# Three prices of the planner's TensorE clock in a two-layer hybrid decoder kernel

## Chip, core and metric

The kernel runs on one core of a Trainium2 chip. The metric is the time of one execution on the device, in microseconds (us); the median of three runs before the change is 1532.54 us.

## What is computed

Two layers over a sequence of 2048 positions and 1024 channels in float32, each of the form x + RMSNorm(mixer(RMSNorm(x))):

```
layer 0:  q,k,v,ga,u,gb = split(h @ w_in)
          ya = sliding_window_attention(q,k,v,sinks) * silu(ga)     # window 128, 8 query heads on 2 kv heads
          yb = multiscale_pool(u) * silu(gb)                        # trailing windows 2, 4, 8, 16
          y  = concat(ya, yb) @ w_out
layer 1:  a,b,gate = split(h @ w_in)                                # 3 x 1024 columns
          glu  = a * sigmoid(b)
          conv = causal_depthwise_conv(glu, 31 taps per channel) + bias
          y    = (silu(layer_norm(conv)) * silu(gate)) @ w_out
```

## The kernel before

**Tiling.** Activations lie with channels on the 128 partitions and positions along the free axis. The sequence is worked in two halves of 1024 positions, a half in two blocks of 512. A weight tile holds 128 output channels against all 1024 input channels (8 tiles of 128 rows). To keep float32's precision with the faster float32r matmuls, weights and activations are split into a high and a low part; a projection of one weight tile on one block (`project`, line 378) is 8 x 3 = 24 matmuls of 512 columns: high times high, high times low, low times high. They sum in one of four "mm" banks of PSUM.

**Stages.** Layer 0, half 0: key, value, query and gate projections with attention beside them, pooling projections, then the output projection (`inproj0`, line 833; `outproj`, 942). The same for half 1. Then layer 1 for either half (`inproj1`, 1173): eight channel tiles with two weights each (the sigmoid's and its partner's), eight gate weights, the output projection. Loads run through SyncE's queue; ScalarE (ACT) makes the high part of a weight and VectorE (DVE) the low part (`w_split`, 348; tiles `wh`, `wl`). There are three buffers for raw weights and two for split ones. Large working tiles come from 37 slots of one tag, `s4`.

**The depthwise convolution.** Of the eight channel tiles, four (0, 1, 3, 5) are convolved on DVE (`conv_dve`, 1021): 31 taps, each one instruction over 1024 positions that multiplies by the channel's tap and adds to an accumulator; in the rows these are `s<-s,packed,s` with 128x1024 elements. The other four (2, 4, 6, 7) are convolved on TensorE (`conv_pe`, 1050): DVE builds a small banded weight tile of 640 elements (`s<-packed,ab`), and five plain float32 matmuls of 128 columns use it (`a<-s,s`, two records each in the trace); there are eight such groups per channel tile. Before that, DVE multiplies the two projections into the convolution's input (`glu`, 1102, `s<-t,mm`). When all eight are done, their sum is made on GpSimd, and a matmul with a tile of ones takes the mean over channels (`norm_block`, 1124, `a<-s,ones`); the layer norm, gate and split follow, and the output projection reads the result.

**What sets the order of the work.** Every engine works through its own queue in the order in which the program issues. This order is found while the program is built, by the class `Flow`. The main stream issues the projections. All else is background work, written as generators that run between the matmuls: `project` calls `flow.pump()` after every three matmuls. `Flow` keeps an estimated clock for each engine (P for TensorE, V for DVE, A for ACT, G, S); `Engine.cost` (lines 153 to 181) gives each instruction a price in us, and `note` advances the clock of its engine by that price, from the time at which its inputs are estimated to be there. `once` lets a background task make its next step under two conditions: the time that the task named as its earliest must lie 0.2 us (`MARGIN`) behind the TensorE clock, and, for a task of any priority but 0, neither the DVE nor the ACT clock may be over 1 us (`LAG`) ahead of the TensorE clock:

```
ready = task[3]
if ready is not None and ready + MARGIN > self.t["P"]:
    continue
if task[0] > 0 and max(self.t["V"], self.t["A"]) > self.t["P"] + LAG:
    continue
```

The DVE convolution is such a background task (priority 4) that offers one tap at a time:

```
for k in range(2, CK):
    yield flow.t["P"]
    r = acc[k % 2]
    V.scalar_tensor_tensor(r, gl[:, k:k + TH], dwn[:, slot, k:k + 1], r, op0=ALU.mult, op1=ALU.add)
```

Weight splits and gate products have priority 0; the convolution matmuls (priority 2) are issued once the TensorE clock has passed the estimated end of the tile that they read. Where the main stream needs something that is not there on the estimate, `wait` advances the TensorE clock. The estimate decides only the order; semaphores hold every real dependency. DVE's prices are 0.063 us + 0.067 us for a per-partition scalar + 1.04 ns per element (half that for plain copies and scalar operations from SBUF).

All instructions are issued through one helper, so that every row of the trace shows its line, L187; rows are told apart by tile names.

Of the kernel before, what the change touches and what calls it, by code (L numbers as in the profile page):

```python
# [49 lines left out]


class Flow:
    """Issues the program in an order that an estimate of each engine's clock suggests.

    Background work is written as generators ("tasks"). A task yields the estimated time at which
    its next step can start, or None when it waits for a buffer or for other tasks. The main stream
    feeds the tensor engine and lets tasks run between its matmuls. Tile draws every dependency;
    the estimate only decides the order of issue.
    """

    def __init__(self):
        self.t = {"P": 0.0, "V": 0.0, "A": 0.0, "G": 0.0, "S": 0.0}
# [7 lines left out]
    def keys(ap):  # L70
# [3 lines left out]
        return [(ap.name, c) for c in range(lo // 256, hi // 256 + 1)]  # L74

    def note(self, e, cost, ins, outs):
        s = self.t[e]
        for x in ins:
# [71 lines left out]
class Engine:  # L150
# [3 lines left out]
    def cost(self, op, out, ins, kw):  # L154
        n = 1
        for d in out.shape[1:]:
            n *= d
        psum = any(x.space == PSUM for x in ins + [out])
        ptr = 0.067 * sum(1 for x in ins if n > 1 and x.shape[-1] == 1)
        if self.key == "P":  # L160
            if op == "transpose":
                return 0.109
            f = ins[0].dtype
            if f == F32R:
                return max(0.107, 0.2148 * n / 512)
            if n * out.shape[0] < 256:
                return 0.108
            part = 0.56 if out.shape[0] == 64 else 1.0
            return part * n * 1.67e-3
        if self.key == "V":  # L170
            if op == "reciprocal":
                return 0.06 + n * 6.25e-3
            fast = op in ("tensor_copy", "tensor_scalar") and not psum
            return 0.063 + ptr + n * (0.52e-3 if fast else 1.04e-3)
        if self.key == "A":
            return (0.052 if psum else 0.093) + 1.4 * ptr + n * 0.833e-3 + (0.09 if kw.get("accum_out") is not None else 0.0)
        if kw.get("op") == ALU.pow:
            return 1.0
        if op == "tensor_tensor":
            return 0.1 + n * 2.2e-3  # L180
        return 0.1 + n * 3.4e-3
# [1122 lines left out]
```

## Time and profile before

| | |
|---|---|
| median of the runs | 1532.54 us (1532.35 to 1534.52) |
| span of the profiled execution | 1531.2 us |
| TensorE matmul, weight load | 1503.7 us, 1227.4 us busy |
| VectorE | 1232.9 us busy |
| ScalarE, GpSimd | 570.3 us, 97.7 us busy |
| instructions | 20024 |

The time of an execution is that of its span and what lies around it; the profiled execution's span is the only part that the profile shows. Busy time is the time in which an engine executes something; matmuls are pipelined, so that a mean of 395 ns for one does not say how often one starts. The granted clock is the share of TensorE's full speed (2.4 GHz) that the chip allowed. In a row of a group, the first number after the bar is busy time, the next the mean of one in ns, and after the second bar stands the engine's idle time just before instructions of that group, with what ended it.

### The profile page before, as it was taken

The numbers are of one execution on the slowest core, as the hardware profiler recorded it, in microseconds if no ns is written. First come the engines' busy times: TensorE is split into PE (matmuls) and PEld (weight loads), VectorE is DVE, ScalarE is ACT, GpSimd is POOL, SyncE is SP. The second block draws the span as 40 slices with busy tenths as digits, with TensorE's granted clock in tenths as the row PEclk, the third lists the DMA queues.
The fourth block names the chain that finished last, engine by engine and source line by source line (L and its number), as shares of the span: only waits on it lengthen the run. The fifth ranks groups of instructions, "written<-read, shape, count | busy, mean of one in ns | idle before, by whom it ended". The sixth has DMA issues, their size and how long they took to land.

```text
span 1531.2 us, 20024 instructions
## 1 busy us (share of the span) xinstructions
PE 1503.7 (98%) x7578; PEld 1227.4 (80%) x7578; DVE 1232.9 (81%) x1913; ACT 570.3 (37%) x1085; POOL 97.7 (6%) x83
## 2 busy tenths in 40 slices
PE   8999999999999999999999999999999999999997
PEld 6877788788877788788888888788888888778897
DVE  7888775787887664686999999887679999998555
ACT  6454432554434432553211121665421111136541
POOL 0000000000000000000202122100000101110000
PEclk9999999999999999999999999999999999999999
DMA  6122211463410011465222122125642122211254
GB/s 221 43 71 84 78 59 55 151 194 124 157 32 32 28 52 45 151 198 175 95 67 66 56 60 74 42 83 166 212 159 66 49 71 63 69 46 42 83 171 145
DMA packets 75695, 146.89 MB, mean 96 GB/s; under 512 B 8144, under 2 KB 31312, under 8 KB 75600
## 3 DMA queue, kind: packets, MB, share of 16 engines
q1 hardware_dynamic: 75600, 145.63, 30.3%
q8 instruction: 59, 0.97, 0.3%
q14 instruction: 36, 0.29, 0.1%
HBM read 118.33 MB, written 18.87 MB: 90 GB/s over the span
## 4 chain that ended last, share of the span: by engine, by line
PE 79%; DVE 16%; issue 3%; DMA 1%; ACT 1%; SPq 0%; POOL 0%; DVEq 0%; POOLq 0%; ACTq 0%
PE mm L187 67%; DVE s L187 14%; PE a L187 6%; PE pv L187 3%; PE pt L187 2%; DVE wl L187 2%; DMA wr<-in_wc 0%; ACT s L187 0%; SPq L187 0%; DMA s<-s 0%; POOL s L187 0%; DMA wr<-in_wa 0%; DVE t L187 0%; ACT wh L187 0%; DVE a L187 0%
## 5 line engine op out<-in xcount | busy, mean ns | idle before, releaser
L187 PE MATMUL mm<-s,wh 128*128 128x512 f32 (+1 forms) x3616 | 1134.3, 395 | 7.3 <-ACT s L187 6.4
L187 PEld LDWEIGHTS mm<-s,wh 128*128 128x128 f32 x3616 | 667.6, 189 | 155.6 <-ACT s L187 8.3
L187 PE MATMUL mm<-s,wl 128*128 128x512 f32 (+1 forms) x1808 | 709.3, 392 | 0.0
L187 PEld LDWEIGHTS mm<-s,wl 128*128 128x128 f32 x1808 | 340.2, 188 | 76.4
L187 DVE SCALAR_TENSOR_TENSOR s<-s,packed,s 128x1024 f32<-128x1024 f32 x232 | 300.9, 1356 | 0.0
L187 ACT ACTIVATE wh<-wr 128x1024 fp32r<-128x1024 f32 (+1 forms) x138 | 145.5, 1054 | 366.3 <-PE mm L187 343.2
L187 DVE TENSOR_TENSOR wl<-wr,wh 128x1024 fp32r<-128x1024 f32 (+1 forms) x138 | 168.0, 1217 | 106.6 <-ACT wh L187 105.3
L187 PE MATMUL a<-s,s 128*128 128x128 f32 (+2 forms) x944 | 131.5, 286 | 6.2 <-DVE s L187 6.1
L187 PEld LDWEIGHTS a<-s,s 128*128 128x128 f32 x944 | 119.9, 191 | 18.0 <-DVE s L187 10.5
L187 ACT ACTIVATE t<-mm 128x512 f32<-128x512 f32 (+1 forms) x122 | 68.7, 563 | 100.2 <-PE mm L187 100.2
L187 DVE TENSOR_TENSOR t<-t,t 128x512 f32<-128x512 f32 (+1 forms) x131 | 86.5, 665 | 18.5 <-ACT t L187 16.7
L187 ACT ACTIVATE s<-mm 128x512 f32<-128x512 f32 (+1 forms) x116 | 68.0, 586 | 57.9 <-PE mm L187 46.1
L187 ACT ACTIVATE s<-t 128x512 fp32r<-128x512 f32 (+1 forms) x52 | 48.9, 939 | 69.0 <-DVE t L187 68.6
L187 POOL TENSOR_TENSOR rs<-ms,mhalf 128x4 f32<-128x4 f32 (+1 forms) x21 | 23.7, 1127 | 731.5 <-DVE ms L187 731.5
L187 DVE TENSOR_TENSOR s<-t,s 128x512 fp32r<-128x512 f32 (+1 forms) x56 | 51.5, 919 | 21.3 <-ACT s L187 19.9
L187 ACT ACTIVATE t<-s 128x512 f32<-128x512 f32 x80 | 48.5, 629 | 52.5 <-DVE s L187 47.1
L187 DVE TENSOR_TENSOR s<-s,s 128x512 f32<-128x512 f32 (+3 forms) x84 | 64.2, 792 | 3.7 <-ACT s L187 2.8
L187 DVE TENSOR_TENSOR t<-pt,packed 128x512 f32<-128x512 f32 x64 | 44.1, 689 | 24.1 <-PE pt L187 23.8
L187 ACT ACTIVATE s<-s,st 128x128 f32<-128x128 f32 x128 | 49.8, 391 | 29.8 <-DVE st L187 29.7
L187 POOL TENSOR_TENSOR s<-s,s 128x1024 f32<-128x1024 f32 x14 | 42.3, 3019 | 285.3 <-DMA s<-t 191.9
L187 ACT ACTIVATE t<-a,packed 128x128 f32<-128x128 f32 x64 | 18.4, 371 | 108.2 <-PE a L187 97.7
L187 DVE TENSOR_TENSOR s<-packed,ab 128x640 f32<-128x640 f32 x64 | 51.6, 851 | 0.0
(104 smaller groups left out, 1018.6 us busy)
## 6 DMA issues: line engine op xcount, KB each, us to landing
wr<-in_wo SPq DMA_DIRECT2D x64, 512.0 KB, 3.5
wr<-in_wc SPq DMA_DIRECT2D x48, 512.0 KB, 3.5
wr<-in_wa SPq DMA_DIRECT2D x27, 512.0 KB, 3.6
xr<-in_xp SPq DMA_DIRECT2D x32, 256.0 KB, 4.0
x<-s SPq DMA_DIRECT2D x32, 256.0 KB, 3.1
xh<-x SPq DMA_DIRECT2D x32, 256.0 KB, 3.0
out_y<-s SPq DMA_DIRECT2D x32, 256.0 KB, 2.4
xr<-x SPq DMA_DIRECT2D x24, 256.0 KB, 3.9
```

The lines of the kernel that those rows point to most:

```text
L187: fn(*args, **kw)
```

## The change

Three prices of TensorE in `Engine.cost` change: a float32r matmul of n columns from 0.2148 x n/512 us (at least 0.107) to 0.007 + 0.224 x n/512 (at least 0.111), and a plain float32 matmul from 1.67 to 1.74 ns per column. The docstring of `Flow` becomes blank lines, so that line numbers stay. The instructions themselves, their sizes and their buffers are untouched.

```diff
--- before.py
+++ after.py
@@ -50,13 +50,13 @@
 
 
 class Flow:
-    """Issues the program in an order that an estimate of each engine's clock suggests.
-
-    Background work is written as generators ("tasks"). A task yields the estimated time at which
-    its next step can start, or None when it waits for a buffer or for other tasks. The main stream
-    feeds the tensor engine and lets tasks run between its matmuls. Tile draws every dependency;
-    the estimate only decides the order of issue.
-    """
+
+
+
+
+
+
+
 
     def __init__(self):
         self.t = {"P": 0.0, "V": 0.0, "A": 0.0, "G": 0.0, "S": 0.0}
@@ -162,11 +162,11 @@
                 return 0.109
             f = ins[0].dtype
             if f == F32R:
-                return max(0.107, 0.2148 * n / 512)
+                return max(0.111, 0.007 + 0.224 * n / 512)
             if n * out.shape[0] < 256:
                 return 0.108
             part = 0.56 if out.shape[0] == 64 else 1.0
-            return part * n * 1.67e-3
+            return part * n * 1.74e-3
         if self.key == "V":
             if op == "reciprocal":
                 return 0.06 + n * 6.25e-3
```

## Rows read from the trace of the kernel before

**Rows 1.** The page, busy us (share of the span) and instructions by engine.
```profile
PE 1503.7 (98%) x7578; PEld 1227.4 (80%) x7578; DVE 1232.9 (81%) x1913; ACT 570.3 (37%) x1085; POOL 97.7 (6%) x83
```

**Rows 2.** The page, chain that ended last, shares of the span by engine.
```profile
PE 79%; DVE 16%; issue 3%; DMA 1%; ACT 1%; SPq 0%; POOL 0%; DVEq 0%; POOLq 0%; ACTq 0%
```

**Rows 3.** Busy by stretch: span, PE, PEld, DVE, ACT, POOL, clock, DMA share, GB/s.
```profile
50.00:200.00 150.00, 149.95 (x903) 116.46 (x902) 128.79 (x379) 74.58 (x222) 2.58 (x5) 1.00 0.21 68
400.00:550.00 150.00, 149.38 (x900) 115.09 (x899) 117.37 (x345) 61.60 (x182) 2.15 (x4) 1.00 0.12 39
736.30:955.60 219.30, 216.56 (x1103) 181.79 (x1102) 217.20 (x195) 38.50 (x69) 37.10 (x20) 1.00 0.24 65
...
1140.80:1360.20 219.40, 215.99 (x1091) 180.24 (x1090) 214.57 (x188) 36.32 (x67) 21.43 (x10) 1.00 0.23 64
```

**Rows 4.** PE's waits, whole run: us in total, times, longest us.
```profile
PE mm L187 <- ACT s L187: 6.4, 3, 5.6
PE a L187 <- DVE s L187: 6.3, 12, 1.3
PE a L187 <- POOL s L187: 2.3, 2, 1.2
```

**Rows 5.** PE's timeline, projections only, 24 matmuls from first to last: start, us.
```profile
599.81 0.39 PE L187 MATMUL mm<-s,wl 128*128 128x512 f32 x1
...
605.36 0.40 PE L187 MATMUL mm<-s,wl 128*128 128x512 f32 x1
```

**Rows 6.** The chain in order of time: start, us, one convolution run of 40 records.
```profile
791.71 4.46 PE a L187 x40
```

**Rows 7.** DVE groups by form, 736.3 to 955.6 us.
```profile
L187 DVE SCALAR_TENSOR_TENSOR s<-s,packed,s 128x1024 f32<-128x1024 f32 x116 | 150.6, 1354 | 0.0
L187 DVE TENSOR_TENSOR s<-packed,ab 128x640 f32<-128x640 f32 x32 | 26.9, 885 | 0.0
L187 DVE TENSOR_TENSOR wl<-wr,wh 128x1024 fp32r<-128x1024 f32 x16 | 19.5, 1222 | 0.6 <-ACT wh L187 0.5
L187 DVE SCALAR_TENSOR_TENSOR s<-t,mm 128x512 f32<-128x512 f32 x14 | 12.3, 880 | 1.3 <-PE mm L187 1.2
L187 DVE TENSOR_SCALAR s<-s,packed 128x1024 f32<-128x1024 f32 x7 | 7.3, 1073 | 0.0
L187 DVE TENSOR_TENSOR s<-s,s 128x1024 f32<-128x1024 f32 x3 | 6.1, 2027 | 0.1
L187 DVE TENSOR_TENSOR t<-t,t 128x512 f32<-128x512 f32 x2 | 1.4, 702 | 0.1
L187 DVE TENSOR_TENSOR s<-s,xr 128x512 f32<-128x512 f32 x2 | 1.3, 710 | 0.0
```

**Rows 8.** PE groups by form, 736.3 to 955.6 us.
```profile
L187 PE MATMUL mm<-s,wh 128*128 128x512 f32 x517 | 161.8, 394 | 0.0
L187 PE MATMUL mm<-s,wl 128*128 128x512 f32 x258 | 101.5, 394 | 0.0
L187 PE MATMUL a<-s,s 128*128 128x128 f32 x320 | 38.3, 277 | 2.7 <-DVE s L187 2.7
```

**Rows 9.** PE groups by form, 1140.8 to 1360.2 us.
```profile
L187 PE MATMUL mm<-s,wh 128*128 128x512 f32 x514 | 161.5, 395 | 0.0
L187 PE MATMUL mm<-s,wl 128*128 128x512 f32 x257 | 101.4, 394 | 0.0
L187 PE MATMUL a<-s,s 128*128 128x128 f32 x320 | 38.2, 277 | 3.4 <-DVE s L187 3.4
```

**Rows 10.** DVE groups by form, 1140.8 to 1360.2 us, taps and gate products.
```profile
L187 DVE SCALAR_TENSOR_TENSOR s<-s,packed,s 128x1024 f32<-128x1024 f32 x116 | 150.3, 1359 | 0.0
...
L187 DVE SCALAR_TENSOR_TENSOR s<-t,mm 128x512 f32<-128x512 f32 x14 | 12.6, 903 | 4.6 <-PE mm L187 4.6
```

**Rows 11.** PE's timeline after the start: start, us; the first 17 matmuls end here.
```profile
13.14 1.05 PE L187 MATMUL mm<-s,wh 128*128 128x512 f32 x2
...
14.42 1.02 PE L187 MATMUL mm<-s,wh 128*128 128x512 f32 x2
```

## The prediction

> **What bounds the kernel now.** First the shares by engine: TensorE (PE) is busy 1503.7 of 1531.2 us, VectorE (DVE) 1232.9 [rows 1]. The chain of waits then runs through PE for 79% of the span and through DVE for 16% [rows 2], so DVE sets the pace somewhere. The busy times by stretch say where: from 736.3 to 955.6 us DVE is busy 217.20 of 219.3 us, from 1140.8 to 1360.2 us 214.57 of 219.4; in the two attention stretches it has 128.79 and 117.37 of 150 [rows 3]. These two stretches, the depthwise convolution of each half, are where both engines are full, cut from its first tap on DVE to the last sum. The waits of PE, last, are small over the whole run: 6.4 us for ACT (5.6 of it in one wait, the start's) and 6.3 us for DVE tiles [rows 4]. A better order could win back little; a worse one can lose much.
>
> The profiled execution's span is 1531.2 us against a median of 1532.54: 1.3 us lie outside the span or between executions, and I add them at the end.
>
> **The change part by part.** No instruction is added, removed or reshaped: the docstring goes, and three prices of the planner rise. What can change is where the background work (DVE, ACT, DMA and their matmuls) stands among the main stream's matmuls.
>
> *The prices against the trace.* In a stretch of nothing but 512-column projections, 24 matmuls take 605.36 - 599.81 = 5.55 us, 0.231 us each [rows 5]. The old price is 0.2148, the new one 0.007 + 0.224 = 0.231: from 7% too low to right. A 128-column float32 matmul stands in the trace as two records; 40 records last 4.46 us, so 0.223 us for one [rows 6]; its price goes from 0.2138 to 0.2227, again right. So the change does what it says for PE.
>
> *The Trainium skill on this.* "TensorE: Matmul & The Clock Gate" (section "Wait — 56ns, not 53.3ns?") gives 215.7 ns from start to start for 512 columns, at the full clock; by it the old price would be the right one. This trace shows 0.231 us [rows 5], and a granted clock of 1.00 in every stretch of [rows 3], so the measurement decides; by the page's pace the term worked out below would be 60 x 0.2157 = 12.9 us where the trace gives 13.9.
>
> *The prices of DVE stay as they are, and they are too low.* A tap of the convolution (1024 elements, one per-partition scalar) is priced 0.063 + 0.067 + 1.065 = 1.195 us; 116 of them keep DVE busy 150.6 us, 1.298 each [rows 7]. The whole first convolution stretch at the planner's prices: 116 x 1.195 = 138.6; 32 weight builds of 640 elements x 0.729 = 23.3; 16 splits x 1.128 = 18.0; 14 gate products x 0.595 = 8.3; 7 first taps at about 0.70 = 4.9; 3 sums x 1.128 = 3.4; 4 of 512 elements x 0.595 = 2.4; together 198.9 us, for 217.2 us of real DVE time [rows 3, 7]. DVE is thus priced 8% too low.
>
> *Both clocks in that stretch.* PE has 517 + 258 = 775 projections and 160 convolution matmuls there [rows 8]: at the old prices 775 x 0.2148 + 160 x 0.2138 = 200.7 us. That is DVE's 198.9 within 1%. The second stretch: 514 + 257 = 771 projections, 160 others [rows 9], 199.8 us on PE's clock; DVE's counts there are those of the first but for one first tap and three short operations fewer [rows 10], where two of them stand, about 196.5 us. This equality is what the rule in `once` enforces: no background step is issued while DVE's clock is over 1 us ahead of PE's. There the throttle binds, and the planner hands out DVE work in exact proportion to its PE clock. Both clocks being 7 to 8% slow, their ratio was nearly right.
>
> *What the new price does there.* The same DVE work, 200.7 us of it with the idle on its clock, is now spread over 200.7 us of PE time at right prices: N x 0.231 + 160 x 0.2227 = 200.7, N = 715 in place of 775. In the order of issue 60 projections move from beside the convolution to behind it, 60 x 0.231 = 13.9 us of PE work; in the second half likewise 13.8. DVE still needs its 217 us. PE can't run ahead: convolution matmuls, and at the end the mean's matmul, are in its one queue at the place where the planner thinks that DVE is done, and each waits for a DVE tile; everything behind it waits too. So PE idles 14 us more per half. Its later work (gate projections, output projection) is as long as before plus the 60 projections, at full pace: nothing after the stretch gives the 14 us back, since PE is 98 to 100% busy there and the waits there are the mean's (2.3 us over both halves, for GpSimd's sum), which depend on DVE's end and not on the order.
>
> What can come off: DVE itself idles 2.1 us in the first stretch and 4.8 in the second [rows 3], mostly for PE's projections before a gate product (1.2 and 4.6) [rows 7, 10]. With DVE always the later one these waits can go, and the stage gets as much shorter. Bounds: 11.8 to 13.9 us for the first half, 9.0 to 13.8 for the second. I take the middle, 12.9 + 11.4 = 24.3 us.
>
> *The attention stretches* (50 to 200 and 400 to 550 us). The same background work now stands beside 7% fewer matmuls: some 140 us of PE in place of 150, in which DVE needs 128.8 and 117.4 us [rows 3]. On average it fits, so the lower bound is nothing. If DVE paced all 300 us, it would be 7% of them, 20 us. PE is busy 149.95 and 149.38 of 150 us there [rows 3], so it waits for nearly nothing now; the nearer end is the low one. I take 3 us for bursts in which the softmax steps run late.
>
> *Loads and the other stretches.* A planned DMA latency is worth 7% fewer matmuls now; the cover is the weight buffers (three raw, two split), and each weight is used for 24 or 48 matmuls, 5.5 or 11 us. Cost nothing; if a load came late the price would be 1 to 2 us once or twice. Below nothing: the start waits are for the first tile and lie ahead of any choice of order, so 1 to 2 us at most can be won outside the convolution. Both ends, -2 to +3, go into the range.
>
> Sum: 24.3 + 3 = 27.3; 1531.2 + 27.3 + 1.3 = 1559.8, rounded to 1560 us.
>
> **Rivals.** (a) *No change.* Buffers, not the throttle, hold the taps back (37 large slots), or the equality of the clocks is chance; then the order hardly moves: 1530 to 1535 us. For it: the code has such waits. Against: two stretches in which the clocks agree within 1 and 2%, while DVE has no idle to show for a missing buffer.
>
> (b) *Faster.* Right prices place the convolution matmuls so that PE meets finished tiles: the waits of PE for DVE in the stretches (2.7 and 3.4 us) [rows 8, 9] and the mean's 2.3 go, 8 us: 1524 us. It decides if DVE's true pace, and not its price, governed how far its work ran ahead of PE. Against it: PE waits for DVE already with the clocks in balance, and the change slows only PE's clock.
>
> (c) *Slower still, by attention*: DVE paces these stretches too, 20 us in place of 3: 1577 us. Its operations on 128 elements cost far more than their price; but PE shows almost no wait there now.
>
> (d) *Slower still, by the clock.* The 14 us per half come in lumps, since between the matmuls of one convolution channel on PE and the next lie up to four weights of 48 projections, 44 us: 8% of that is 3.5 us of idle. After the idle start the first 17 matmuls ran at the 1.2 GHz level, at (14.42 - 13.14) / 3 = 0.427 us [rows 11], 0.196 us over the full pace, 3.3 us in all. If every lump brought that back, a slow PE would only wait less at the next group, as DVE sets the pace; what stays is the last lump of each half: 7 us, 1567. The Trainium skill ("TensorE: Matmul & The Clock Gate", section "Why this matters for your kernels") has idle gaps between bursts bring the half clock back; the granted clock is 1.00 in all stretches of [rows 3], and PE's longest wait for DVE is 1.3 us [rows 4], so this trace shows neither such a gap nor its price.
>
> **How the numbers follow.** Forecast 0.72, (a) 0.09, (b) 0.07, (c) 0.06, (d) 0.06. A change under 0.2% (3 us) can't be told from none. Faster is (b), 0.07; same is (a), 0.09; the rest is slower, 0.84. The forecast's own range is 1551 to 1571: 20.8 us for both stretches with nothing from attention and 2 us won, up to 27.7 with 8 from attention and 3 from loads. To leave out no more than 2 in 10 I reach down to 1541, for a throttle that binds for part of the stretch only, and up to 1577 for (c) and (d).
>
> **What would show it.** Right: the convolution stretches keep DVE's busy time (about 217 and 215 us) and hold some 60 projections fewer each; PE's waits for DVE and its idle time there grow from 3 to about 14 us, ahead of convolution matmuls; the stages behind them grow in matmuls, not in waits. Wrong: counts of projections beside the taps as before (then (a)); longer waits between 50 and 200 us (then (c)); a granted clock under 1.00 between the convolution groups (then (d)); a shorter stretch with the same 116 taps would overthrow the working altogether.

## The result and the profile after

The changed kernel takes 1574.14 us (median; 1573.01 to 1575.61) beside 1532.66 for the kernel before in the same measurement: 2.7% slower, ratio 1.0269 with the interval [1.0254, 1.0283]. Forecast were 1560 us and a loss of 27; the loss is 41.5. Span of the profiled execution: 1573.8 us.

Busy times by engine and the chain's shares by engine, from the page of the changed kernel:
```profile
PE 1521.0 (97%) x7578; PEld 1236.8 (79%) x7578; DVE 1229.2 (78%) x1913; ACT 569.6 (36%) x1085; POOL 104.0 (7%) x83
...
PE 67%; DVE 24%; issue 4%; DMA 3%; ACT 2%; SPq 0%; POOL 0%; DVEq 0%; POOLq 0%; ACTq 0%
```
The instructions are the same in number [rows 1]; the chain runs through DVE for 24% of the span where it was 16% [rows 2].

Where the time went can be read from the main stream, whose order is fixed: the start of its nth projection matmul (counted from 0) in either trace (us, worked out from the start times):
```
projection   stands at                      before    after    late
 672         half 0's attention done          234.4    239.8     5.4
1824         half 1's attention done          558.3    569.0    10.7
2592         first taps of convolution 1      740.8    753.1    12.3
3552         behind convolution 1            1009.0   1037.2    28.1
4320         before convolution 2            1190.4   1218.7    28.3
5184         behind convolution 2            1437.4   1479.7    42.3
5711         the last                        1518.4   1560.8    42.4
```
So 10.7 us are lost with the two attention stretches, 1.6 more on the way to the first convolution, 15.8 and 14.0 in the convolutions, and nothing in between. Such differences hold to about 1 us: the start alone, up to the 48th projection, put two kernels whose layer 0 was left as before 0.9 us ahead in their traces.

The stretches of [rows 3] in the changed kernel (the convolutions from the first tap to the start of the last DVE sum, as there):
```profile
50.00:200.00 150.00, 147.27 (x880) 112.97 (x879) 122.40 (x366) 70.37 (x216) 2.54 (x5) 1.00 0.21 67
400.00:550.00 150.00, 147.58 (x887) 112.70 (x887) 113.62 (x349) 60.65 (x181) 1.41 (x3) 1.00 0.14 43
749.10:966.80 217.70, 207.19 (x1018) 173.93 (x1017) 212.33 (x194) 34.44 (x61) 41.18 (x19) 0.96 0.22 62
1168.80:1380.80 212.00, 200.70 (x989) 167.90 (x988) 207.98 (x184) 31.45 (x55) 18.55 (x9) 0.98 0.22 61
```
In the convolutions PE is now idle for 10.5 and 11.3 us, where it was 2.7 and 3.4, and its granted clock is under 1.00 for the first time. PE's longest waits over the run, answering [rows 4]:
```profile
PE a L187 <- DVE s L187: 25.1, 16, 4.6
PE mm L187 <- ACT s L187: 7.0, 3, 5.9
PE pt L187 <- DVE t L187: 2.4, 3, 1.5
PE a L187 <- POOL s L187: 2.2, 2, 1.1
...
PE pv L187 <- DVE t L187: 1.9, 5, 0.5
```
The first row is the change: convolution matmuls (`a`) waited 6.3 us for DVE's tiles and now wait 25.1, up to 4.6 at once. PE's groups in the first convolution, then in the second, to be held against [rows 8, 9]:
```profile
L187 PE MATMUL mm<-s,wh 128*128 128x512 f32 x474 | 149.9, 397 | 0.0
L187 PE MATMUL mm<-s,wl 128*128 128x512 f32 x238 | 94.4, 396 | 0.0
L187 PE MATMUL a<-s,s 128*128 128x128 f32 x298 | 41.0, 303 | 9.0 <-DVE s L187 9.0
```
```profile
L187 PE MATMUL mm<-s,wh 128*128 128x512 f32 x474 | 148.2, 394 | 0.0
L187 PE MATMUL mm<-s,wl 128*128 128x512 f32 x238 | 93.7, 394 | 0.0
L187 PE MATMUL a<-s,s 128*128 128x128 f32 x277 | 36.9, 297 | 11.3 <-DVE s L187 11.2
```
712 projections stand beside either convolution, where 775 and 771 stood; the forecast had 715 for the first. One of the waits, in PE's timeline (start, duration), and then the stretches of the wait and behind it (the granted clock is the third number from the end):
```profile
917.25 0.62 PE L187 MATMUL mm<-s,wh 128*128 128x512 f32 x2
917.71 0.40 PE L187 MATMUL mm<-s,wl 128*128 128x512 f32 x1
922.55 7.51 PE L187 MATMUL a<-s,s 128*128 128x128 f32 x40 [4.44 <-DVE s L187]
929.81 0.71 PE L187 MATMUL mm<-s,wh 128*128 128x512 f32 x2
```
```profile
917.70:922.40 4.70, 0.41 (x2) 0.00 (x0) 4.70 (x5) 0.00 (x0) 0.96 (x1) 0.91 0.41 70
922.40:928.40 6.00, 5.85 (x27) 5.85 (x28) 6.00 (x8) 0.00 (x0) 3.51 (x1) 0.50 0.24 87
```
PE has nothing to do for 4.4 us, the granted clock falls to 0.50, the 1.2 GHz level, and the 40 records behind the wait take 7.3 us instead of 4.46 [rows 6]. DVE is busy throughout.

The convolution does not end with the last DVE sum. Up to the mean's matmul, the two stages of the kernel before and then of the changed one:
```profile
736.37:960.21 223.84, 220.02 (x1117) 184.30 (x1115) 219.15 (x196) 39.72 (x71) 39.48 (x21) 1.00 0.23 64
1140.83:1364.86 224.03, 219.40 (x1105) 182.67 (x1103) 216.61 (x189) 36.29 (x67) 23.78 (x11) 1.00 0.23 63
```
```profile
749.15:976.86 227.71, 216.07 (x1067) 181.28 (x1065) 214.24 (x195) 36.07 (x66) 45.93 (x21) 0.96 0.22 60
1168.81:1397.35 228.54, 213.91 (x1066) 178.77 (x1064) 214.94 (x188) 34.23 (x64) 23.62 (x11) 0.98 0.22 59
```
The stages are 3.9 and 4.5 us longer, though they hold 50 and 40 projections fewer.

### The profile page after: what moved, and what is told of

It is laid out like the page before. It is cut to its first block, busy times and chain, and to the rows that moved or that the text cites. A ratio compares the mean times of both kernels' runs of the same rounds, so it can differ in the third digit from the quotient of the medians.

```text
span 1573.8 us, 20021 instructions
## 1 busy us (share of the span) xinstructions
PE 1521.0 (97%) x7578; PEld 1236.8 (79%) x7578; DVE 1229.2 (78%) x1913; ACT 569.6 (36%) x1085; POOL 104.0 (7%) x83
## 4 chain that ended last, share of the span: by engine, by line
PE 67%; DVE 24%; issue 4%; DMA 3%; ACT 2%; SPq 0%; POOL 0%; DVEq 0%; POOLq 0%; ACTq 0%
PE mm L187 55%; DVE s L187 20%; PE a L187 7%; PE pv L187 3%; PE pt L187 2%; DVE wl L187 2%; DVE t L187 2%; ACT s L187 1%; ACT t L187 1%; DMA xr<-in_xp 1%; DMA xh<-in_xn 0%; DMA xr<-x 0%; DMA s<-in_xn 0%; SPq L187 0%; DMA wr<-in_wc 0%
## 5 line engine op out<-in xcount | busy, mean ns | idle before, releaser
L187 DVE SCALAR_TENSOR_TENSOR s<-s,packed,s 128x1024 f32<-128x1024 f32 x232 | 293.3, 1328 | 0.0
L187 PE MATMUL a<-s,s 128*128 128x128 f32 (+2 forms) x944 | 142.6, 301 | 25.1 <-DVE s L187 24.3
L187 PEld LDWEIGHTS a<-s,s 128*128 128x128 f32 x944 | 129.6, 205 | 39.4 <-DVE s L187 28.7
L187 DVE TENSOR_TENSOR s<-t,s 128x512 fp32r<-128x512 f32 (+1 forms) x56 | 51.4, 918 | 23.1 <-ACT s L187 22.1
L187 ACT ACTIVATE t<-a,packed 128x128 f32<-128x128 f32 x64 | 18.3, 369 | 122.4 <-PE a L187 122.4
```

Of the source, the lines that this page charges most:

```text
L187: fn(*args, **kw)
```

## Experiments

Beside each result stands how late four projections are against the kernel before: 1824 (behind attention), 2592 (ahead of convolution 1), 3552 (behind it), 5184 (behind convolution 2). In the changed kernel: 10.7, 12.3, 28.1, 42.3.

**The convolution's DVE prices.**
```diff
+            if op == "scalar_tensor_tensor" and n == TH and ptr:
+                return 1.298
+            if op == "scalar_tensor_tensor" and n == BL and psum and len(out.shape) == 3 and not ptr:
+                return 0.88
+            if op == "tensor_tensor" and n == TH and len(out.shape) == 3 and out.shape[1] == SG:
+                return 2.03
```


> The changed kernel, with three DVE operations of the convolution priced as they lasted in the trace of before: a tap 1.298 us in place of 1.195, a gate product 0.88 in place of 0.595, the last sum of a channel 2.03 in place of 1.13. Theory (the throttle hands out DVE work in proportion to TensorE's clock, so the ratio of the two prices decides): the 30 us lost in the two convolutions come back, the 11 us of the attention stretches stay: 1543 us, down to 1535 if the waits of before go too; PE waits under 2 us per convolution channel and keeps a granted clock of 1.00. Rival (TensorE's price itself spoils the order, through the 0.2 us margin or the planned loads): no gain, 1565 us or more.

1537.94 us, ratio 1.0033 [1.0022, 1.0045]; late by 9.3, 10.7, 9.3, 3.3. Its two convolution stretches (here with the last sum, 2.0 us), and PE's wait in the first:
```profile
747.40:970.00 222.60, 221.64 (x1126) 186.16 (x1125) 218.62 (x197) 39.72 (x71) 48.37 (x20) 1.00 0.23 64
1149.40:1368.90 219.50, 219.50 (x1116) 184.83 (x1114) 215.69 (x189) 36.95 (x68) 25.06 (x10) 1.00 0.22 64
```
```profile
L193 PE MATMUL a<-s,s 128*128 128x128 f32 x320 | 37.6, 276 | 1.0 <-DVE s L193 1.0
```
With TensorE's new prices untouched, the convolutions lose nothing: they even win 1.4 and 6.0 us over the kernel before. There a right price of PE does no harm beside right prices of DVE; the rival falls. The attention stretches still lose 9.3 us.

**New prices in layer 0 only.**
```diff
-                return max(0.111, 0.007 + 0.224 * n / 512)
+                return max(0.111, 0.007 + 0.224 * n / 512) if self.flow.layer == 0 else max(0.107, 0.2148 * n / 512)
...
+    flow.layer = 1
     for half in range(NH):
         mix, done = inproj1(half, hs, have)
```
(The plain float32 price likewise.)

> The new TensorE prices in layer 0 only, the old ones from the first projection of layer 1 on. Theory (two separate losses, 10.7 us up to the end of layer 0's attention and 30 us in the two convolutions): 1532.7 + 10.7 = 1543 us, and convolution stretches as before. Rival (the order of layer 0 sets up the loss in layer 1): 1560 us or more.

1544.62 us, ratio 1.0078 [1.0062, 1.0093]; late by 8.7, 10.5, 10.8, 10.8. With the old prices in layer 1 the convolutions lose at most 0.3 us: layer 0's order does not set up their loss. The new TensorE prices in layer 1 alone were not run.

**The ratio alone.**
```diff
-            return 0.063 + ptr + n * (0.52e-3 if fast else 1.04e-3)
+            return 0.93 * (0.063 + ptr + n * (0.52e-3 if fast else 1.04e-3))
```
(In the kernel before; the reciprocal's price likewise.)

> The kernel before, its TensorE prices untouched, with every DVE price multiplied by 0.93: the ratio of the changed kernel with the old TensorE price. Theory (the ratio decides): some 45 projections move behind each convolution and the time is near the changed kernel's, 1560 to 1576 us. Rival (a right TensorE price is what does harm, not the ratio): 1531 to 1537 us.

1567.93 us, ratio 1.0227 [1.0211, 1.0242]; late by 4.5, 5.7, 24.7, 35.7. PE's groups in its first convolution:
```profile
L187 PE MATMUL mm<-s,wh 128*128 128x512 f32 x478 | 149.4, 394 | 0.0
L187 PE MATMUL mm<-s,wl 128*128 128x512 f32 x239 | 93.9, 393 | 0.0
L187 PE MATMUL a<-s,s 128*128 128x128 f32 x280 | 37.2, 297 | 12.3 <-DVE s L187 12.2
```
Without any change of TensorE's prices, 717 projections are left beside the taps and the same waits appear: 19.0 and 11.0 us for the two convolutions. What decides there is the ratio of the prices of DVE and TensorE. The attention stretches lose 4.5 us and not 10.7; here ACT's prices kept their old ratio to TensorE's.

**Half the lead.**
```diff
-LAG = 1.0
+LAG = 0.5
```


> The changed kernel with a LAG of 0.5 us in place of 1.0. Theory (a rate is wrong, not an offset): the convolutions lose as much as in the changed kernel, 28 to 32 us against before; in all 1568 to 1580 us. Rival (DVE work is let in too far ahead, and a smaller lead would mend it): 1555 us or less.

1569.38 us, ratio 1.0239 [1.0224, 1.0254]; late by 8.1, 9.7, 23.1, 34.4. The total is in the expected range, the convolutions' part is smaller than expected: 24.7 us for 28 to 32. The lead matters a little; most of the loss stays, as a rate and not an offset. Both conditions of `once` compare with the TensorE clock; a kernel without the throttle was not run, so how much each of the two does is not shown.

**Extra work in the wait.**
```diff
+            if r == 0:
+                for _ in range(WARM):
+                    nc.tensor.matmul(bk[:, :P], identr, khc[0], start=True, stop=True)
             for j in range(NJ):
```
(In the changed kernel, WARM = 24.)

> The changed kernel with 24 extra matmuls of 128 columns (constants, results overwritten, unknown to the planner, so that the order stays) ahead of the first convolution group of each channel that TensorE convolves: about 2.7 us of work in the place where TensorE waited 3.5 to 4.8 us and its clock then fell to 1.2 GHz. Theory (part of the loss is the slow clock after the wait): the granted clock stays at 1.00 in the convolutions, and the time falls by 4 to 8 us, to 1566 to 1570 us. Rival (DVE paces these stretches, so a slow TensorE costs nothing there): 1574 to 1578 us with the clock at 1.00.

1572.76 us, ratio 1.0260 [1.0244, 1.0275], which overlaps the changed kernel's interval; late by 9.6, 11.0, 26.4, 39.8. Its two convolutions (with the last sum):
```profile
747.50:966.10 218.60, 215.63 (x1125) 183.58 (x1123) 213.79 (x195) 34.41 (x61) 38.09 (x19) 0.98 0.23 62
1166.40:1380.10 213.70, 209.88 (x1092) 177.93 (x1091) 209.96 (x185) 31.62 (x56) 18.15 (x9) 0.99 0.22 61
```
The mean clock rose from 0.96 and 0.98 to 0.98 and 0.99, not to 1.00: two of the five falls are gone. The time hardly moved. The expected 4 to 8 us did not come; with half of the slow time removed, the clock's part can't be told from nothing. The extra matmuls are work too, and what of it fell outside the waits is not shown. What the clock's part would be with all falls removed stays open.

**Without the GpSimd sums**, in the changed kernel and in the kernel before:
```diff
-        elif len(made) > 2:
-            yield G.tensor_tensor(out=cfs["sum"], in0=cfs["sum"], in1=cf, op=ALU.add)
```


> The changed kernel without six of the seven GpSimd additions per half that sum the convolved channels (the mean is then that of two channels and its matmul waits for these alone). In the trace of before a tap lasts 1.196 us, its price, when GpSimd does not add, and up to 3.4 us when it does: some 12 us per half. Theory (DVE is short of its prices mostly because of these additions): DVE needs 12 us less per half beside the same order, PE's waits shrink by as much, 1550 us (1545 to 1554). Rival (taps slow for another reason, or the loss is not DVE's): 1568 us or more.

The sums are not made when all eight channels are done, as the kernel's description above has it: `add_conv` issues one on GpSimd as each channel from the second on ends, so that most run beside the taps.

1547.53 us, ratio 1.0094 [1.0079, 1.0109]; late by 10.3, 11.9, 13.1, 13.1: the convolutions lose nearly nothing. Its two stretches (with the last DVE sum, 2.0 us):
```profile
748.50:954.90 206.40, 202.36 (x1032) 168.69 (x1031) 205.81 (x195) 34.42 (x61) 30.75 (x15) 1.00 0.24 66
1153.80:1356.80 203.00, 198.83 (x996) 165.10 (x996) 201.60 (x185) 32.20 (x58) 10.99 (x5) 1.00 0.23 64
```
DVE's work is 205.81 - 2.0 = 203.8 and 199.6 us in place of 212.3 and 208.0, 8.5 us less in each, and PE's idle time falls from 10.5 and 11.3 us to 4.0 and 4.2. The edit does one thing more: the mean's matmul no longer waits for the last channel. But 13.3 and 11.0 us are gone ahead of the last DVE sum already (217.7 - 204.4 and 212.0 - 201.0).

> The kernel before without the same six additions per half. Theory: DVE, no longer behind its prices, waits for PE; only PE's own waits of 4 to 6 us per half go: 1523 to 1528 us, and the gap between this kernel and the changed one without additions is 15 to 25 us in place of 41. Rival: as much is won as in the changed kernel, 1510 us or less, and the gap stays at 41 us.

1520.42 us, ratio 0.9917 [0.9903, 0.9932]; late by -0.9, -0.9, -6.5, -13.1. Its stretches, again with the last sum:
```profile
735.70:949.50 213.80, 213.80 (x1098) 180.84 (x1097) 208.56 (x196) 38.27 (x69) 17.40 (x15) 1.00 0.25 67
1134.90:1347.70 212.80, 212.80 (x1085) 179.31 (x1084) 206.14 (x189) 35.25 (x65) 7.30 (x5) 1.00 0.24 66
```
DVE needs 206.5 and 204.1 us, 10.7 and 10.4 less than in [rows 3], and PE has no idle left. More was won than expected, and the gap to the changed kernel without sums is 27.1 us, just over the expected 15 to 25, against 41 with the sums. Of the convolutions' 30 us some 13 are left in the gap (1.2 and 0 lost on one side, 5.6 and 6.6 won on the other): of DVE's shortfall against its prices in the first stretch, 217.2 - 198.9 = 18.3 us, the six additions are 10.7; 7.6 remain, among them gate products (0.88 us for 0.595) and permuted sums (2.03 for 1.128), whose prices are too low.

**Layer 0's prices.** The first experiment's kernel, with
```diff
+            if op == "tensor_tensor_reduce":
+                return 0.30
+            if op == "tensor_tensor" and n == BL and len(out.shape) == 3 and out.shape[1] == BL // PH:
+                return 1.005
...
+            if n == BL and len(out.shape) == 3 and out.shape[1] == BL // PH:
+                return 0.94
```
(the last for ACT).

> The kernel with the convolution's DVE prices of the first experiment (1537.94 us), and three prices of layer 0 as the trace of before has them: the score reduction 0.30 us in place of 0.196, the permuted low part of a mixed tile 1.005 in place of 0.595, its high part on ACT 0.94 in place of 0.52. Theory (the 9 to 11 us of the attention stretches are the same ratio): most of it comes back, 1528 to 1532 us. Rival (the attention stretches lose for another reason): 1536 to 1540 us.

1530.43 us, ratio 0.9985 [0.9975, 0.9995]; late by 1.6, 2.9, 1.1, -4.3. Of the first experiment's 9.3 us in attention 7.7 are gone. The loss there too lay mostly in the prices of DVE and ACT beside a dearer TensorE; which of the three prices matters was not tried.

**Old prices in layer 0, new prices with the three DVE prices in layer 1.**

> Old TensorE prices in layer 0; in layer 1 the new ones with the three DVE prices of the first experiment (a tap 1.298 us, a gate product 0.88, the last sum 2.03). Theory (losses and gains of the two layers add): no attention loss, and the 5 to 7 us that the convolutions gained in the first experiment against before: 1525 to 1529 us, faster than before. Rival (the layers don't add): 1532 to 1538 us.

1525.70 us, ratio 0.9956 [0.9942, 0.9969]; late by 0.1, 0.1, -2.1, -7.6: 0.4% faster than the kernel before, in the expected range: the gains of the convolutions stand without layer 0's loss.

**The sums on DVE.** On top of that:
```diff
-            yield G.tensor_tensor(out=cfs["sum"], in0=cfs["sum"], in1=cf, op=ALU.add)
+            yield V.tensor_tensor(out=cfs["sum"], in0=cfs["sum"], in1=cf, op=ALU.add)
```
(The first sum likewise; the mean waits for DVE's clock in place of GpSimd's, and a tap is priced 1.20 in place of 1.298.)

> As the kernel with both prices, but the channel sums of the convolution are made on DVE (1.13 us each by their price) in place of GpSimd, and a tap is priced 1.20. Theory (a GpSimd sum costs DVE about 1.7 us in stalled taps, 12 us per half for seven): seven sums on DVE cost 8 us per half, and the mean no longer waits for GpSimd: 3 to 8 us better than the kernel with both prices, 1518 to 1524 us. Rival (the stall of the taps is not GpSimd's doing): 8 us per half worse than it, 1540 us or more.

1522.76 us, ratio 0.9936 [0.9923, 0.9948]; late by -0.9, -0.9, -5.1, -11.9: the fastest of the kernels that leave nothing out, 2.9 us under the one before it for 3 to 8 expected. How much of that is the lower price of a tap was not tried. All its taps:
```profile
L194 DVE SCALAR_TENSOR_TENSOR s<-s,packed,s 128x1024 f32<-128x1024 f32 x232 | 282.9, 1275 | 0.0
```
1.219 us each, for 1.297 in the kernel before (150.6 + 150.3 us for 232) [rows 7, 10].

## Why the prediction came out as it did

**The direction and the mechanism held.** The planner ties DVE's share to TensorE's clock: 712 projections are left beside the taps where the working gave 715; a DVE price 7% lower does the same harm (1567.93 us) with the old TensorE price; right DVE prices in the convolution undo it under the new one (1537.94). PE's one queue turned DVE's lateness into waits ahead of convolution matmuls, as forecast, and nothing behind the stretch gave them back. Rivals (a) and (b) are out.

**The convolution's term was too small by 5.5 us:** 24.3 forecast, 29.8 measured. The step that failed is the credit for DVE's idle time, "with DVE always the later one these waits can go, and the stage gets as much shorter", and with it the premise that the mean's wait depends "on DVE's end and not on the order". Up to the mean's matmul DVE idles 13.5 and 13.6 us, where it idled 4.7 and 7.4. One part is the gate products: in the first stretch DVE waits 5.2 us for their projections, where it waited 1.2 [rows 7], likely because PE, behind a wait, has to catch up:
```profile
L187 DVE SCALAR_TENSOR_TENSOR s<-t,mm 128x512 f32<-128x512 f32 x14 | 12.4, 886 | 5.2 <-PE mm L187 5.2
```
The larger part is the end, which moved: now a channel convolved on TensorE comes last, and its result goes through a DMA to GpSimd's last sum, while DVE idles (start, us):
```profile
968.84 2.39 POOL L187 TENSOR_TENSOR s<-s,s 128x1024 f32<-128x1024 f32 x1 [11.02 <-DVE s L187]
974.44 2.37 POOL L187 TENSOR_TENSOR s<-s,s 128x1024 f32<-128x1024 f32 x1 [3.21 <-DMA s<-t]
```
So ahead of the mean's matmul only 50 and 40 projections are missing, 11.6 and 9.2 us at 0.231, and the mean itself is 3.9 and 4.5 us later: 15.5 and 13.7, the loss of the two stretches (15.8 and 14.0).

**One sign that should have overthrown the working came true.** The prediction named it: "a shorter stretch with the same 116 taps". From the first tap to the last DVE sum it is 217.7 and 212.0 us, where it was 219.3 and 219.4, and DVE's busy time there is 212.3 and 208.0 and not the expected 217 and 215. The sign was badly chosen, since the stretch ends before the stage does. In the second half four of the 32 weight builds now stand behind the last DVE sum:
```profile
1380.77 2.00 DVE L187 TENSOR_TENSOR s<-s,s 128x1024 f32<-128x1024 f32 x1
1382.61 5.16 DVE L187 TENSOR_TENSOR s<-packed,ab 128x640 f32<-128x640 f32 x4
```
And fewer taps run into a GpSimd sum (below): five of the 232 last over 3.4 us, where eight did. "DVE still needs its 217 us" was wrong by that much; the stage as a whole is longer.

**The attention's term was mis-sized:** 3 us taken, 10.7 measured, within the bounds of 0 and 20. The step was the choice of the low end, from PE's lack of waits before. That row showed that PE did not wait, not how little it would take to make it wait: three prices are too low by a third to a half (0.196 for 0.30, 0.595 for 1.005, 0.52 for 0.94). With them mended 7.7 of 9.3 us are gone; that DVE and ACT run late there in bursts is argued, not shown. Rival (c) had the reason, operations dearer than their price, and twice the size. The other stretches, taken at nothing, cost 1.6 us ahead of the first convolution; the cause is open.

**The total was partly luck.** Both terms were too small, and 1574.14 us lies near the upper end of the range, 1577, which was set for (c) and (d) and not for a larger convolution term.

**Rival (d)** described what happens: waits in lumps, and a clock of 0.50 behind them. PE idles only 7.8 and 10.0 us more up to the mean, not the working's 14 per half; the rest of what it lost is pace. Its work shrank by 11.6 and 9.2 us of projections, its busy time by 4.0 and 5.5 us; a mean clock of 0.96 and 0.98 over these stages stands for some 9 and 5 us, an estimate that about covers the difference. But (d)'s price of 7 us in the whole was not found: with half the slow time gone, the time fell by 1.4 us, inside the intervals. DVE paces these stretches, so a slower PE may only shorten its own next wait; that is argued, not shown. Its row from the start was also read too low: 0.427 us holds for the last nine of the 17 matmuls. The first starts at 5.57 us and the 16th at 14.42, with 0.5 us of idle between, 0.56 us each:
```profile
5.57 1.58 PE L187 MATMUL mm<-s,wh 128*128 128x512 f32 x2 [5.57 <-ACT s L187]
```

**"DVE is priced 8% too low" was right as a sum and wrong as a reading.** I took it as the operations' own cost. The kernel before shows otherwise; first DVE, then GpSimd (start, us):
```profile
1347.31 8.46 DVE L187 SCALAR_TENSOR_TENSOR s<-s,packed,s 128x1024 f32<-128x1024 f32 x7
...
1356.81 3.44 DVE L187 SCALAR_TENSOR_TENSOR s<-s,packed,s 128x1024 f32<-128x1024 f32 x1
```
```profile
1356.18 2.99 POOL L187 TENSOR_TENSOR s<-s,s 128x1024 f32<-128x1024 f32 x1 [30.63 <-DMA s<-t]
```
Seven taps in a row start 1.20 us apart, the planner's 1.195; the one that runs beside GpSimd's sum takes 3.44. Without six of the seven sums DVE needs 10.7 us less in the first stretch of the kernel before, so more than half of the 18.3 us that its prices lack there is this contention. No price per operation can hold it, since it depends on what runs beside.

## What to carry to other kernels

A planner that throttles one engine's work by another engine's clock is governed by the ratio of their prices. Correcting one side alone can be worse than leaving both wrong by the same share; add up both sides' prices over a stretch, and both engines' real time, before touching one. Where the sums of the throttled engine fall short, look in the timeline for what runs beside its slow instances: moving that work, with a tap's price lowered to match, gave 3 us here on top of right prices (1525.70 to 1522.76). And a stretch without waits says nothing of how much cover is left. A stretch that is cut at one engine's last instruction can get shorter while the stage gets longer: cut it where the next stage starts.

## What the runs showed of the hardware

A GpSimd addition of two 128x1024 float32 tiles can hold up the DVE tap beside it: eight taps of the kernel before took 3.42 to 3.44 us, where taps in a row start 1.20 us apart. Not each addition does: beside one in the changed kernel the taps kept their pace, five in 6.07 us, and the addition took 4.84 us:
```profile
818.02 6.07 DVE L187 SCALAR_TENSOR_TENSOR s<-s,packed,s 128x1024 f32<-128x1024 f32 x5
```
```profile
821.52 4.84 POOL L187 TENSOR_TENSOR s<-s,s 128x1024 f32<-128x1024 f32 x1 [15.09 <-DMA s<-t]
```
With the additions on DVE the taps' mean fell from 1.297 to 1.219 us. The Trainium skill ("GPSIMD Engine Reference", section "1. Specifications") lists the SBUF interfaces as shared between GpSimd and VectorE, with contention when a DVE instruction has two inputs in SBUF; a tap has two, and the trace agrees.

TensorE's granted clock fell to 0.50 five times in the convolutions of the changed kernel. Four falls stand at waits of 3.4 to 4.6 us; the first stands behind a shorter one and eight matmuls of one column:
```profile
755.47 1.05 PE L187 MATMUL pt<-ones,t 128*128 128x1 f32 x8 [1.50 <-DVE t L187]
```
```profile
757.74:761.15 3.41, 3.41 (x10) 2.63 (x9) 3.41 (x6) 0.00 (x0) 1.98 (x1) 0.50 0.43 154
```
In the kernel before, waits of up to 1.3 us in the same stretches left it at 1.00, and in the changed kernel one of 1.50 us ahead of convolution matmuls did too. The Trainium skill ("TensorE: Matmul & The Clock Gate", section "Why this matters for your kernels") has idle gaps between bursts of matmuls do this; the trace agrees as to the fall. Work put into the waits took away half of the slow time and moved the whole by 1.4 us, inside the intervals.
